# Two more 8 KB load tiles in a hybrid layer kernel, room taken from GpSimd's descriptor ring and from small tiles

## The chip, the cores and the metric

The kernel runs on one core of one Trainium2 chip. The metric is device time in microseconds (us) of one launch. Engines are called by the profile's names: PE (TensorE, with PEld for its weight loads), DVE (VectorE), ACT (ScalarE), POOL (GpSimd) and SP (SyncE, which here only issues DMAs). All weights lie in device memory as float32 and are read once.

## The reference

One layer of a diffusion backbone over 512 latent tokens and 256 context tokens of width 1024. Cut to what matters:

```
m  = silu(c) @ w_mod + b_mod                       # 6 vectors: shift, scale, gate, twice
h  = rmsnorm(x, g1) * (1 + scale1) + shift1        # the same for ctx
u  = h @ w_in                                      # q, k, v (512 each) | hyena (768) | conformer (512)
na = neighbourhood_attention(q, k, v, k_ctx, v_ctx, rpb)   # 8 heads, 8x16 window + 256 context keys
hy = hyena_mixer(u_hy)                             # short conv, two long convs by FFT, gates
cf = conformer_conv(u_cf)                          # GLU, 31-tap conv, layer norm, silu
x  = x + gate1 * (concat(na, hy, cf) @ w_out)
h  = rmsnorm(x, g2) * (1 + scale2) + shift2
# 16 experts, each takes its top 64 tokens by softmax affinity
aff = softmax(h @ w_router);  gate, idx = top_k(aff.T, 64)
y_e = (silu(h[idx] @ w1[e]) * (h[idx] @ w3[e])) @ w2[e]    # 1024 -> 2048 -> 1024
x  = x + gate2 * scatter_add(gate * y_e, idx)
out = rmsnorm(x, final_norm_g)
```

## The kernel before

**Load tiles.** A pool `big` holds `NU` = 22 tiles of 128 partitions x 2048 float32 (8 KB a partition, 1 MB in all). Every weight piece is loaded into such a tile, and many intermediate results (rows of x, the halves of split weights, mixer outputs `mixh`, `mixl`, the bias table `tm`) take one too. `U()` (L65) hands a tile out; a counter `used` may not go over `NU`. The loads stand in one list, `loads`, in a fixed order: adaLN and input-projection pieces by a string of letters (L227), the two halves of the k projection, then `w_out` and the rows of x (L252), adaLN group 3 (L259), and from L261 on for each expert eight pairs `w1`, `w3` and eight `w2`. `pump` (L72) issues from the head of that list while fewer than `NU` tiles are in use (less a reserve, `keep`); it is called where the code gives tiles back (`free`). All of these loads go out from SP's one queue in this order (`load`, L162). Since the pool goes round, a load waits on the chip for the last readers of the tile that it gets.

**Stages.** (1) to about 96 us: adaLN groups and the transposed, normalised x. (2) 96 to 262 us: the input projections. For exactness, weights and activations are split into a high and a low float32r part (`split`: ACT L515 makes `wh`; POOL or DVE, L516, makes `wl`), and three products are summed on PE (`mm3`, L548 to L550). Between them lie the hyena mixer (PE L698 in the DFT's space, DVE L685 to L707, POOL L685) and the conformer branch (DVE L583 GLU, L590 the 31-tap conv in 60 instructions, then the layer norm whose first matmuls are PE `pL` L598, and DVE `mixl` L562 at its end). (3) Attention: scores (PE `pS` L932, DVE L940, ACT L943), transposes (L952), values (L963), with the output projection's matmuls (`pX`) and routing laid between by a written order of PE's instructions. The keys `KK` are copied out of PSUM by L105 (DVE) and L103 (ACT). The upper half of `w_out` is multiplied by the gate vector `g1bc` on DVE (L867, four instructions a tile) as it comes in. The bias table is made by POOL (L849) from pieces that POOL itself loads (`fetch_bias`, L841). (4) The experts: PE L1305 and L1306 (`pa`, w1 and w3), L1333 transposes, L1346 (`py`, w2); gather and scatter are matmuls too (L1182, L1202). (5) The end: last scatter, final norm, output by 4 DMAs and one indirect DMA of POOL for the rows of the last expert (L1373).

In stages 1 and 2 a scheduler sets the order of instructions on each engine; its order depends on when it thinks a load arrives. From the start of attention on, PE's order is written out by hand.

Of the kernel before, what the change touches and what calls it, by code (L numbers as in the profile page):

```python
# [9 lines left out]
FT = mybir.dt.float32  # L10
FR = mybir.dt.float32r
I32 = mybir.dt.int32
U32 = mybir.dt.uint32
# [9 lines left out]
CAP = 64  # L23
FF = 2048
EPS = 1e-6
NU = 22
RPBW = 63


# [21 lines left out]
def hybrid_kernel(ctx: ExitStack, tc: tile.TileContext, a, out: bass.AP):  # L51
    nc = tc.nc
# [59 lines left out]
    ident = c1[:, C1["id"]]  # L112
    bmod = early.tile([32, 512], FT, name="bmod")
    nc.scalar.dma_start(bmod, a["bmod"])
    eps = small.tile([128, 1], FT, name="eps")
    nc.vector.memset(eps, EPS)
    one256 = small.tile([128, 1], FT, name="one256")
    nc.vector.memset(one256, 1.0 / 256.0)
    ones = one256.to_broadcast([128, 128])
    g1bc = small.tile([128, D], FT, name="g1bc")  # L120
# [12 lines left out]
    pair = small.tile([128, 64], FT, name="pair")  # L133
    nc.vector.tensor_add(pair, ident[:, 0:64], ident[:, 64:128])

    def small_t(name, n, dt=FT, bufs=4):
        return work.tile([128, n], dt, name=name, tag=name, bufs=bufs)

    def rsqrt_mean(dst, ss, n, scale=1.0 / D):
# [127 lines left out]
            load(("w2", e, j), a["w2"][e, j * 256:(j + 1) * 256].rearrange("(p k) n -> p (k n)", k=2))  # L267


    def norm_rows(rows, junk, n, ss, name):  # L270

        for i in range(n):
            nc.scalar.activation(junk[i], rows[i], AF.Square, accum_out=ss[:, i:i + 1])
        rs = small.tile([128, n], FT, name=name)
        rsqrt_mean(rs, ss[:, :n], n)
        for i in range(n):
            nc.vector.tensor_scalar(rows[i], rows[i], rs[:, i:i + 1], None, op0=OP.mult)
# [50 lines left out]
    nc.vector.tensor_sub(h2s[64:128], h2f[64:128], h2s[64:128].bitcast(FT))  # L328
    free_only(1)
    xn = [take(("x", 0)), take(("x", 1))]  # L330
    ss = small.tile([128, 4], FT, name="ssx")
    hr = [U("hr0"), U("hr1")]
    pump(6)
    half = lambda t, i: t[:, i * D:(i + 1) * D]
    norm_rows([half(xn[b // 2], b % 2) for b in range(4)], [half(hr[b // 2], b % 2) for b in range(4)], 4, ss, "rsx")

    def transpose_rows(src, n, dst):

# [437 lines left out]
    def ctx_prep():  # L776
        cx = take("ctx")
        rows = [half(cx, i) for i in range(2)]
        ssc = small.tile([128, 2], FT, name="ssc")
        hcr = U("hcr")  # L780
        norm_rows(rows, [half(hcr, i) for i in range(2)], 2, ssc, "rsc")
        yield
        v256 = hcr.rearrange("p (k n) -> p k n", n=256)
        for _ in transpose_rows(rows, 2, lambda k4, i: v256[:, 4 * k4:4 * k4 + 4, 128 * i:128 * i + 128]):
            pass
        free_only(1)
        yield
        cmod = modulate_split(lambda k: v256[:, k], 256, 1, "hc")
        kv["hc"] = next(cmod)
        finish(cmod)  # L790
        free_only(1)
        yield
# [123 lines left out]
    xblk = lambda b: xr[b // 2][:, (b % 2) * D:(b % 2 + 1) * D]  # L916

    tok = c1[:, C1["tok"]]
    ssq = small.tile([128, 4, 2], FT, name="ssq")

    affT = g1bc[0:16, 0:512].rearrange("e (i n) -> e i n", i=2)
    idxf = p1[0:16, 0:128].rearrange("e (i n) -> e i n", i=2)
    rsT = small.tile([128, 4], FT, name="rsT")

    def scores(hp, b):

        k0 = 8 * KB[b]
        o = 768 * (hp % 2) + k0
        kk = KK[hp // 2][:, o:o + 2 * (512 - k0)].rearrange("p (a n) -> p a n", a=2)[:, :, 0:256]
        pss = [psA("pS") for _ in range(2)]  # L930
        for s in range(2):
            mm(pss[s].rearrange("p (a n) -> p a n", a=2), Q[0][HALF[s], hp, 128 * b:128 * b + 128], kk[HALF[s]],  # L932
               start=True, stop=True)
        out = []
        for s, ps in enumerate(pss):
            p = W("P")
            i = 2 * TYPE[b] + s
            m2 = small_t("m2", 4, bufs=6)

            nc.vector.tensor_tensor_reduce(out=p.rearrange("p (a n) -> p a n", a=2), in0=ps.rearrange("p (a n) -> p a n", a=2),  # L940
                                           in1=TM[hp][:, i:7:6 - i], scale=1.0, scalar=3e38,
                                           op0=OP.add, op1=OP.min, accum_out=m2[:, 0:1])
            nc.scalar.activation(p, p, AF.Exp, scale=-1.0, bias=m2[:, 0:1], accum_out=m2[:, 1:2])  # L943
            nc.vector.reciprocal(m2[:, 2:3], m2[:, 1:2])
            nc.vector.tensor_scalar(p, p, m2[:, 2:3], None, op0=OP.mult)
            out.append(p)
        return out
# [68 lines left out]
    def route(b):  # L1016
        eng = nc.vector if b in () else nc.gpsimd
        s1 = small_t("s1", 1)
        eng.tensor_add(s1, ssq[:, b, 0:1], ssq[:, b, 1:2])
        rs = rsT[:, b:b + 1]  # L1020
        v, t, y = small_t("rv", 1), small_t("rt", 1), small_t("ry", 1, I32)
        yf = y.bitcast(FT)
        eng.tensor_scalar(v, s1, 1.0 / D, EPS, op0=OP.mult, op1=OP.add)
        eng.tensor_scalar(y, v.bitcast(I32), -0.5, 1597463007.0, op0=OP.mult, op1=OP.add)
        eng.tensor_scalar(v, v, -0.5, None, op0=OP.mult)
        for i in range(3):
            eng.tensor_scalar(t, yf, yf, v, op0=OP.mult, op1=OP.mult)
            eng.tensor_scalar(rs if i == 2 else yf, t, 1.5, yf, op0=OP.add, op1=OP.mult)
        x_rows(b, 1)
        yield  # L1030
        pl = psY("pR")
        for k4 in range(2):
            for k in range(4):
                mm(pl[32 * k:32 * k + 32, 0:128], rwA[:, 4 * k4 + k], xTr[b, k4][:, k * 128:(k + 1) * 128],
                   start=(k4 == 0), stop=(k4 == 1))
        lt = W("lt")[:, 0:128]
        nc.scalar.activation(lt, pl[:, 0:128], AF.Copy)
        yield
        p2 = psY("pR")
        mm(p2[:, 0:16], lt, rsum, start=True, stop=True)  # L1040
        lg = small_t("lg", 16, bufs=2)
        nc.vector.scalar_tensor_tensor(lg, p2[:, 0:16], rs, rwB, op0=OP.mult, op1=OP.add)

        mx = small_t("mx", 1)
        nc.vector.tensor_reduce(out=mx, in_=lg, axis=AX.X, op=OP.min)
        ex = small_t("ex", 16, bufs=2)
        sm_ = small_t("sme", 2)
        nc.scalar.activation(ex, lg, AF.Exp, scale=-1.0, bias=mx, accum_out=sm_[:, 0:1])
        nc.vector.reciprocal(sm_[:, 1:2], sm_[:, 0:1])
        nc.vector.tensor_scalar(ex, ex, sm_[:, 1:2], None, op0=OP.mult)  # L1050
        yield
        p3 = psY("pR")
        nc.tensor.transpose(p3[0:16, 0:128], ex, ident)
        c = slice(16 * (b % 2), 16 * (b % 2) + 16)
        nc.vector.tensor_copy(affT[:, b // 2].rearrange("e (r c) -> e c r", c=32)[:, c], cr(p3[0:16, 0:128]))
# [169 lines left out]
    pi = psY("pI")  # L1225
    nc.tensor.transpose(pi[:, 0:16], idxf.rearrange("e a b -> e (a b)"), ident[0:16, 0:16])
    nc.tensor.transpose(pi[:, 16:32], vals.rearrange("e a b -> e (a b)"), ident[0:16, 0:16])
    fng = rwA.rearrange("p k e -> p (k e)")[0:8, 0:128]
    ig = small.tile([128, 32], FT, name="ig")
    nc.vector.tensor_copy(ig, pi[:, 0:32])  # L1230
    nc.gpsimd.dma_start(fng, a["fng"].rearrange("(r p) -> r p", p=128))
    prev = None
# [2 lines left out]

    def final_rows():

        s2 = small.tile([128, 4, 2], FT, name="s2")
        s1 = small.tile([128, 4], FT, name="s1f")
        rs = small.tile([128, 4], FT, name="rsf")  # L1240
        e = E - 1
        pb = psY("pB")
        mm(pb[:, 0:64], ident[0:16, e:e + 1].to_broadcast([16, 128]), idxf[:, 0], start=True, stop=True)
# [12 lines left out]
        for h in range(2):  # L1256
            p = psT("pB")
# [9 lines left out]
        for h in range(2):  # L1267
            nc.vector.tensor_add(pairs[:, 64 * h:64 * h + 64], ident[:, 0:64], ident[:, 64:128])

        where = small.tile([128, 4], U32, name="where")  # L1270
        nc.vector.tensor_copy(where[:, 0:1], ig[:, e:e + 1])
        for i, (bits, shift) in enumerate(((31, 1), (224, 2))):
            nc.vector.tensor_scalar(where[:, i + 1:i + 2], where[:, 0:1], bits, shift,
# [195 lines left out]
```

## Time and profile before

| what | value |
|---|---|
| time, median of 3 runs | 1343.46 us (1341.08 to 1345.36) |
| profiled execution: its own time | 1341.92 us |
| profiled execution: span of the trace | 1340.1 us |
| mean granted TensorE clock | 0.985 |
| PE busy | 1255.4 us (94%) |
| DVE, ACT, POOL busy | 505.7, 223.9, 156.5 us |
| DMA traffic | 457.99 MB, mean 342 GB/s |

The span is what the trace covers; 1.8 us lie around it. A busy share is an average over the whole span: PE's 94% says only that few stages leave it idle, not that PE sets the end of each. In the strip of 40 slices below, one slice is 33.5 us long.

### The profile page before, as it was taken

What the parts mean: (1) busy time and instruction counts of PE and PEld (TensorE: products, weight loads), DVE (VectorE), ACT (ScalarE), POOL (GpSimd) and SP (SyncE); (2) the same over time, 40 slices, a digit from 0 to 9 for tenths busy, and PEclk for the clock granted to TensorE, in tenths of its full rate; (3) what the DMA queues carried; (4) which work ended last, traced back from release to release, by engine and by line L of the source; (5) the groups of instructions that cost most, each with busy time, mean ns of one, the idle gap of its engine ahead of it and who ended that gap; (6) DMA issues with size and microseconds to landing.
All of it is one profiled execution on the core that took longest, in us unless ns stands there. A gap on an engine that the chain in (4) does not pass through costs nothing.

```text
span 1340.1 us, 14779 instructions
## 1 busy us (share of the span) xinstructions
PE 1255.4 (94%) x5916; PEld 578.9 (43%) x5916; DVE 505.7 (38%) x1034; ACT 223.9 (17%) x480; POOL 156.5 (12%) x166
## 2 busy tenths in 40 slices
PE   6898988989979999999999999999999999999997
PEld 2576567856644333333333334343333334343332
DVE  6877998478571131221312122121211212121224
ACT  3532232335520110101101011010101001010103
POOL 2333444546110000000000000000000000000000
PEclk9998999989989999999999999999999999999999
DMA  9934214534367999999999999999999999999996
GB/s 344 375 138 162 77 63 118 190 127 185 139 270 276 421 422 421 422 421 421 421 420 420 422 421 421 421 421 421 421 421 421 422 421 421 421 421 422 421 420 256
DMA packets 72979, 457.99 MB, mean 342 GB/s; under 512 B 7364, under 2 KB 9228, under 8 KB 21710
## 3 DMA queue, kind: packets, MB, share of 16 engines
q1 hardware_dynamic: 71662, 453.64, 83.4%
q0 software_dynamic: 912, 3.06, 0.9%
q8 instruction: 46, 0.75, 0.2%
q10 hardware_dynamic: 336, 0.35, 0.1%
q14 instruction: 23, 0.19, 0.0%
HBM read 453.87 MB, written 2.36 MB: 340 GB/s over the span
## 4 chain that ended last, share of the span: by engine, by line
PE 49%; DMA 35%; DVE 13%; issue 2%; ACT 1%; POOLq 0%; SPq 0%; DVEq 0%; ACTq 0%
DMA ld<-in_w_dram 33%; PE pa L1305 18%; PE py L1346 7%; DVE glu L590 4%; PE pZ L1202 3%; PE pG L1182 2%; PE pP L550 1%; PE pP L548 1%; PE pP L549 1%; PE pS L932 1%; PE pO L963 1%; PE pM L431 1%; PE pX L548 1%; PE pX L549 1%; PE pX L550 1%
## 5 line engine op out<-in xcount | busy, mean ns | idle before, releaser
L1306 PE MATMUL pa<-ld,xh 128*64 128x512 f32 x1024 | 463.8, 597 | 14.7 <-DMA ld<-in_w_dram 14.7
L1305 PE MATMUL pa<-ld,xh 128*64 128x512 f32 x1024 | 466.4, 597 | 0.3 <-DVE xh L1062 0.3
L1346 PE MATMUL py<-ld,xh 128*64 128x512 f32 x1024 | 223.3, 594 | 0.0
L1305 PEld LDWEIGHTS pa<-ld,xh 128*64 128x64 f32 x1024 | 131.6, 136 | 199.1 <-issue 191.2
L1205 DVE TENSOR_TENSOR acc<-acc,pZ 128x512 f32<-128x512 f32 x112 | 73.2, 685 | 288.7 <-PE pZ L1202 288.2
L1306 PEld LDWEIGHTS pa<-ld,xh 128*64 128x64 f32 x1024 | 132.2, 137 | 102.5 <-issue 65.1
L1346 PEld LDWEIGHTS py<-ld,xh 128*64 128x64 f32 x1024 | 72.1, 137 | 139.3 <-issue 136.9
L1373 POOL DMA_INDIRECT out_dram<-yg,where x1 | 1.1, 1097 | 932.0 <-DVE yg L1372 932.0
L1060 ACT ACTIVATE xh<-pT,B,A 128x64 f32<-128x64 f32 (+1 forms) x60 | 24.4, 406 | 443.1 <-PE pT L1190 334.3
L1350 DVE SCALAR_TENSOR_TENSOR yg<-py,ig,g1bc 128x512 f32<-128x512 f32 x16 | 12.0, 752 | 205.0 <-PE py L1346 205.0
L1202 PE MATMUL pZ<-yg,oh 64*128 64x512 f32 x240 | 84.4, 640 | 4.8 <-DVE acc L1205 3.9
L516 POOL TENSOR_TENSOR wl<-ld,wh 128x512 fp32r<-128x512 f32 x44 | 64.5, 1493 | 81.7 <-ACT wh L515 42.0
L548 PE MATMUL pP<-hh,wh 128*128 128x512 f32 x144 | 59.0, 411 | 1.2 <-ACT hh L505 1.2
L550 PE MATMUL pP<-hh,wl 128*128 128x512 f32 x144 | 57.2, 405 | 2.7 <-DVE wl L516 2.7
L549 PE MATMUL pP<-hl,wh 128*128 128x512 f32 x144 | 57.0, 397 | 1.5 <-DVE hl L507 1.5
L590 DVE SCALAR_TENSOR_TENSOR glu<-glu,p 128x512 f32<-128x512 f32 x60 | 56.9, 949 | 1.1
L1333 PE MATMUL pT<-c,au 128*128 128x128 f32 x256 | 47.4, 312 | 6.2 <-DVE xh L1336 2.2
L1182 PE MATMUL pG<-ld,ohg 128*64 128x512 f32 x224 | 52.8, 592 | 0.0
L1202 PEld LDWEIGHTS pZ<-yg,oh 64*128 64x128 f32 x240 | 22.7, 184 | 65.6 <-issue 35.7
L103 ACT ACTIVATE xg<-pG 128x512 f32<-128x512 f32 x7 | 4.2, 597 | 279.3 <-PE pG L1182 279.3
L1062 DVE TENSOR_SCALAR xh<-pT,A,B 128x64 f32<-128x64 f32 (+1 forms) x60 | 20.7, 344 | 73.5 <-ACT xh L1060 28.5
L1333 PEld LDWEIGHTS pT<-c,au 128*128 128x128 f32 x256 | 35.7, 208 | 26.9 <-DVE acc L1205 12.5
(345 smaller groups left out, 1353.7 us busy)
## 6 DMA issues: line engine op xcount, KB each, us to landing
ld<-in_w_dram SPq DMA_DIRECT2D x384, 1024.0 KB, 19.8
ld<-in_w_mod_dram SPq DMA_DIRECT2D x24, 1024.0 KB, 14.2
ld<-in_w_in_dram SPq DMA_DIRECT2D x11, 1024.0 KB, 5.5
ld<-in_w_out_dram SPq DMA_DIRECT2D x4, 1024.0 KB, 5.1
ld<-in_x_dram SPq DMA_DIRECT2D x2, 1024.0 KB, 12.4
ld<-in_x_dram SPq DMA_DIRECT2D x4, 512.0 KB, 6.7
out_dram<-acc SPq DMA_DIRECT2D x4, 512.0 KB, 9.3
g<-in_rpb_dram POOLq DMA_DIRECT2D x8, 244.5 KB, 6.1
```

Of the source, the lines that this page charges most:

```text
L516: (nc.vector if i in dve else nc.gpsimd).tensor_sub(lo[:, s], raw[:, s], hi[:, s].bitcast(FT))
L548: mm(ps, l[0], r[0], start=start, stop=False)
L549: mm(ps, l[0], r[1], start=False, stop=False)
L550: return mm(ps, l[1], r[0], start=False, stop=stop)
L590: nc.vector.scalar_tensor_tensor(yc[i], glt[i][:, j:j + 512], cw[:, i, j:j + 1], yc[i], op0=OP.mult, op1=OP.add)
L1182: mm(pg[64 * h:64 * h + 64], g[:, 64 * b:64 * b + 64], xblk(b)[:, 512 * h:512 * h + 512], start=(b == 0), stop=(b == 3))
L1202: mm(ps[h], oh[pr, 128 * c:128 * c + 128], yg[pr], start=True, stop=True)
L1205: nc.vector.tensor_add(ablk(c)[:, s], (ablk if e else xblk)(c)[:, s], ps[h])
L1305: mm(pa[f][0:64], xT[:, k, cs], w1[:, s], start=(k == 0), stop=(k == 7))
L1306: mm(pa[f][64:128], xT[:, k, cs], w3[:, s], start=(k == 0), stop=(k == 7))
L1333: nc.tensor.transpose(p[:, i * 128:(i + 1) * 128], au[f][:, c:c + 255:2], ident)
L1346: mm(py[64 * h:64 * h + 64], hT[:, f], w2[:, i * 1024 + 512 * h:i * 1024 + 512 * h + 512], start=(f == 0), stop=(f == 15))
```

## The change

The pool gets 24 tiles instead of 22. Room for the 16 KB comes from four places: the ring in which GpSimd writes the descriptors of its own DMAs is set to 1 KB a partition; single-column statistics go into one array `stat` (128x32) or into unused columns of `rwA`, where each had a tile of its own; small scalar tiles have 2 buffers instead of 4 (`m2` 5 instead of 6); and the router's exponentials are written over the logits.

```diff
-NU = 22
+NU = 24
...
-    eps = small.tile([128, 1], FT, name="eps")
+    stat = small.tile([128, 32], FT, name="stat")
+    eps, one256 = stat[:, 0:1], stat[:, 1:2]
...
-    def small_t(name, n, dt=FT, bufs=4):
+    def small_t(name, n, dt=FT, bufs=2):
...
-    ss = small.tile([128, 4], FT, name="ssx")
+    ss = stat[:, 4:8]
...
-    ssq = small.tile([128, 4, 2], FT, name="ssq")
+    ssq = stat[:, 16:24].rearrange("p (b n) -> p b n", n=2)
...
-            m2 = small_t("m2", 4, bufs=6)
+            m2 = small_t("m2", 4, bufs=5)
...
-        ex = small_t("ex", 16, bufs=2)
+        ex = lg
...
-    fng = rwA.rearrange("p k e -> p (k e)")[0:8, 0:128]
-    ig = small.tile([128, 32], FT, name="ig")
+    rwf = rwA.rearrange("p k e -> p (k e)")
+    fng, ig = rwf[0:8, 0:128], rwf[:, 128:160]
...
-        s2 = small.tile([128, 4, 2], FT, name="s2")
-        s1 = small.tile([128, 4], FT, name="s1f")
-        rs = small.tile([128, 4], FT, name="rsf")
+        s2 = rwf[:, 160:168].rearrange("p (c h) -> p c h", h=2)
+        s1, rs = rwf[:, 168:172], rwf[:, 172:176]
...
-    nc = _bacc.Bacc("TRN2", target_bir_lowering=False, num_devices=1)
+    nc = _bacc.Bacc("TRN2", target_bir_lowering=False, num_devices=1, dynamic_dma_scratch_size=1024)
```

Each engine has the same instructions as before, in the same number. The order differs in stage 2 and at its border with attention. Lines of the changed kernel are one lower there (L866 is L867 of before).

At the start of attention, DVE before; `ld` is a `w_out` tile, `pC` and `pP` hold the keys of the context and of the latent tokens:

```order
L618 TENSOR_TENSOR glu<-glu,pL 128x512 x2
L105 COPY KK<-pC 128x256
L562 TENSOR_TENSOR mixl_1175<-glu,mixh_1174 128x512 x2
L105 COPY KK<-pC 128x256
L105 COPY KK<-pP 128x512
L867 TENSOR_TENSOR ld<-ld,g1bc 128x512 x8
L105 COPY KK<-pP 128x512
```

DVE at the same place in the changed kernel:

```order
L617 TENSOR_TENSOR glu<-glu,pL 128x512 x2
L866 TENSOR_TENSOR ld<-ld,g1bc 128x512 x4
L561 TENSOR_TENSOR mixl_1172<-glu,mixh_1171 128x512
L105 COPY KK<-pC 128x256
L561 TENSOR_TENSOR mixl_1172<-glu,mixh_1171 128x512
L105 COPY KK<-pC 128x256
L866 TENSOR_TENSOR ld<-ld,g1bc 128x512 x4
L105 COPY KK<-pP 128x512 x2
```

The first tile's four gate products now stand ahead of `mixl`, the second tile's four after it; both copies of the latent keys still end the group.

SP's queue at the `w_out` loads, before; in brackets stand the semaphores waited for (DMAHW ones are SP's own lanes, the others name the engine that read the tile last):

```order
L162 DMA ld<-in_w_out_dram 128x4x512 [waits DVE_49]
L162 DMA ld<-in_w_out_dram 128x4x512 [waits DMAHW3_49,PE_49,Pool_49]
L162 DMA ld<-in_w_out_dram 128x4x512 [waits DMAHW4_49,PE_49]
L162 DMA ld<-in_w_mod_dram 128x2x1024 [waits DMAHW5_49,PE_49]
L162 DMA ld<-in_w_mod_dram 128x2x1024 [waits DMAHW6_49,PE_49]
```

The same five loads in the changed kernel:

```order
L162 DMA ld<-in_w_out_dram 128x4x512 [waits DMAHW2_49,PE_49]
L162 DMA ld<-in_w_out_dram 128x4x512 [waits DMAHW3_49,PE_49]
L162 DMA ld<-in_w_out_dram 128x4x512 [waits DVE_49,DMAHW4_49,PE_49,Pool_49]
L162 DMA ld<-in_w_mod_dram 128x2x1024 [waits DMAHW5_49,PE_49]
L162 DMA ld<-in_w_mod_dram 128x2x1024 [waits DMAHW6_49,DVE_49]
```

The wait for DVE that stood ahead of the first of three `w_out` loads now stands ahead of the third.

In stage 2, DVE before, around the first long conv of the hyena branch (L687 to L689 finish the spectrum `Y`, L516 makes a low half of a weight):

```order
L685 TENSOR_TENSOR t<-pH,KM 128x512 x2
L516 TENSOR_TENSOR wl<-ld,wh 128x512 x2
L687 TENSOR_TENSOR t<-t 128x512 x2
L640 SCALAR_TENSOR_TENSOR hx<-u,p_70,hx 128x511
L687 TENSOR_TENSOR t<-t 128x512
L688 TENSOR_TENSOR Y<-t 128x256
L689 TENSOR_TENSOR Y<-t 128x256
```

The changed kernel there:

```order
L515 TENSOR_TENSOR wl<-ld,wh 128x512 x2
L684 TENSOR_TENSOR t<-pH,KM 128x512 x2
L639 SCALAR_TENSOR_TENSOR hx<-u,p_70,hx 128x511
...
L640 SCALAR_TENSOR_TENSOR hx<-u,p_70,hx 128x511
L686 TENSOR_TENSOR t<-t 128x512 x2
L687 TENSOR_TENSOR Y<-t 128x256
```

The two `wl` stand ahead of the products with `KM` now, and the first `Y` follows its two L686 directly. PE's order in stage 2 moved with it: four more projection matmuls stand ahead of the L698 group that needs this `Y`, and the second `pL` (L598) stands 13 matmuls earlier among the projections.

## Rows read from the trace of the kernel before

**Rows 1.** The page: GB/s in 40 equal slices of the span.

```profile
GB/s 344 375 138 162 77 63 118 190 127 185 139 270 276 421 422 421 422 421 421 421 420 420 422 421 421 421 421 421 421 421 421 422 421 421 421 421 422 421 420 256
```

**Rows 2.** The page: the chain that ended last, by engine.

```profile
PE 49%; DMA 35%; DVE 13%; issue 2%; ACT 1%; POOLq 0%; SPq 0%; DVEq 0%; ACTq 0%
```

**Rows 3.** Windows: PE, PEld, DVE, ACT, POOL busy, granted clock, DMA share, GB/s.

```profile
400.00:442.00 42.00, 40.32 (x204) 18.13 (x204) 7.92 (x32) 2.43 (x5) 1.05 (x1) 1.00 0.72 285
...
835.00:1276.00 441.00, 423.90 (x1810) 162.18 (x1810) 85.47 (x174) 31.81 (x76) 0.00 (x0) 1.00 1.01 421
```

**Rows 4.** Issues of SP's queue from 395 us on, and median issue to landing.

```profile
411.00 56.72 SPq L162 DMA_DIRECT2D ld<-in_w_dram  x27
...
ld<-in_w_dram SPq DMA_DIRECT2D x384, 1024.0 KB, 19.8
```

**Rows 5.** PE's timeline at its last wait for a weight of the experts.

```profile
1275.97 0.64 PE L1306 MATMUL pa<-ld,xh 128*64 128x512 f32 x1 [1.32 <-DMA ld<-in_w_dram]
```

**Rows 6.** The chain from 215 to 300 us, into attention: start, us, what.

```profile
225.99 0.68 DVE vc L105
226.67 0.60 DVE wl L516
...
233.23 0.23 PE pP L550
...
252.52 12.21 DMA ld<-in_w_out_dram
```

**Rows 7.** DVE's timeline from 248 to 271 us.

```profile
248.87 2.59 DVE L562 TENSOR_TENSOR mixl<-glu,mixh 128x512 fp32r<-128x512 f32 x2
...
260.75 2.50 DVE L867 TENSOR_TENSOR ld<-ld,g1bc 128x512 f32<-128x512 f32 x4 [2.78 <-DMA ld<-in_w_out_dram]
264.75 5.38 DVE L867 TENSOR_TENSOR ld<-ld,g1bc 128x512 f32<-128x512 f32 x4 [1.49 <-DMA ld<-in_w_out_dram]
270.06 0.68 DVE L105 COPY KK<-pP 128x512 f32<-128x512 f32 x1
```

**Rows 8.** SP: issue of the last `w_out` loads, their wait, their median to landing.

```profile
251.49 1.47 SPq L162 DMA_DIRECT2D ld<-in_w_out_dram  x3
...
SPq L162 <- DVE mixl L562: 30.9, 1, 30.9
...
ld<-in_w_out_dram SPq DMA_DIRECT2D x4, 1024.0 KB, 5.1
```

**Rows 9.** PE's timeline at the start of attention.

```profile
262.61 1.13 PE L932 MATMUL pS<-KK,Q 64*128 64x512 f32 x4
...
266.31 0.39 PE L550 MATMUL pX<-wh,mixl 128*128 128x512 f32 x1
270.79 2.68 PE L932 MATMUL pS<-KK,Q 64*128 64x512 f32 x4 [4.09 <-DVE KK L105]
```

**Rows 10.** The window behind that wait, columns as in rows 3.

```profile
270.80:277.50 6.70, 6.70 (x19) 4.61 (x20) 5.90 (x18) 3.52 (x9) 0.33 (x1) 0.53 0.28 75
```

**Rows 11.** PE's waits from 96 to 265 us: sum, times, longest.

```profile
PE pH L698 <- DVE Y L688: 4.3, 2, 3.9
PE pL L598 <- DVE glu L590: 3.4, 1, 3.4
```

**Rows 12.** Windows behind those two waits, columns as in rows 3.

```profile
109.80:116.60 6.80, 5.85 (x19) 3.29 (x20) 3.34 (x11) 0.00 (x0) 0.01 (x1) 0.50 0.51 168
229.20:232.70 3.50, 3.50 (x18) 3.40 (x17) 2.31 (x4) 1.26 (x2) 0.00 (x0) 0.51 0.00 0
```

**Rows 13.** DVE's timeline from 126 to 135 us, in the conformer branch.

```profile
126.69 1.07 DVE L583 TENSOR_TENSOR glu<-pP,sig 128x512 f32<-128x512 f32 x1 [3.14 <-PE pP L550]
...
132.52 1.77 DVE L516 TENSOR_TENSOR wl<-ld,wh 128x512 fp32r<-128x512 f32 x1
```

**Rows 14.** GpSimd's own DMAs: the page's queue row, and POOL's timeline behind two loads.

```profile
q0 software_dynamic: 912, 3.06, 0.9%
...
249.41 3.38 POOL L849 TENSOR_TENSOR tm<-c,g 128x256 f32<-128x256 f32 x3 [2.53 <-DMA g<-in_rpb_dram]
```

More of the change, by code (lines that the diff above doesn't have):

```diff
@@ L114, in hybrid_kernel @@
     nc.scalar.dma_start(bmod, a["bmod"])
-    eps = small.tile([128, 1], FT, name="eps")
+    stat = small.tile([128, 32], FT, name="stat")
+    eps, one256 = stat[:, 0:1], stat[:, 1:2]
     nc.vector.memset(eps, EPS)
-    one256 = small.tile([128, 1], FT, name="one256")
     nc.vector.memset(one256, 1.0 / 256.0)
@@ L267, in hybrid_kernel, with norm_rows @@
             load(("w2", e, j), a["w2"][e, j * 256:(j + 1) * 256].rearrange("(p k) n -> p (k n)", k=2))
-    def norm_rows(rows, junk, n, ss, name):
+    def norm_rows(rows, junk, n, ss, rs):
         for i in range(n):
             nc.scalar.activation(junk[i], rows[i], AF.Square, accum_out=ss[:, i:i + 1])
-        rs = small.tile([128, n], FT, name=name)
         rsqrt_mean(rs, ss[:, :n], n)
@@ L334, in hybrid_kernel @@
     half = lambda t, i: t[:, i * D:(i + 1) * D]
-    norm_rows([half(xn[b // 2], b % 2) for b in range(4)], [half(hr[b // 2], b % 2) for b in range(4)], 4, ss, "rsx")
+    norm_rows([half(xn[b // 2], b % 2) for b in range(4)], [half(hr[b // 2], b % 2) for b in range(4)], 4, ss, stat[:, 8:12])
     def transpose_rows(src, n, dst):
@@ L778, in ctx_prep @@
         rows = [half(cx, i) for i in range(2)]
-        ssc = small.tile([128, 2], FT, name="ssc")
+        ssc = stat[:, 12:14]
         hcr = U("hcr")
-        norm_rows(rows, [half(hcr, i) for i in range(2)], 2, ssc, "rsc")
+        norm_rows(rows, [half(hcr, i) for i in range(2)], 2, ssc, stat[:, 14:16])
         yield
@@ L918, in hybrid_kernel @@
     tok = c1[:, C1["tok"]]
-    ssq = small.tile([128, 4, 2], FT, name="ssq")
+    ssq = stat[:, 16:24].rearrange("p (b n) -> p b n", n=2)
     affT = g1bc[0:16, 0:512].rearrange("e (i n) -> e i n", i=2)
     idxf = p1[0:16, 0:128].rearrange("e (i n) -> e i n", i=2)
-    rsT = small.tile([128, 4], FT, name="rsT")
+    rsT = stat[:, 24:28]
     def scores(hp, b):
@@ L1268, in final_rows @@
             nc.vector.tensor_add(pairs[:, 64 * h:64 * h + 64], ident[:, 0:64], ident[:, 64:128])
-        where = small.tile([128, 4], U32, name="where")
+        where = rwf[:, 176:180].bitcast(U32)
         nc.vector.tensor_copy(where[:, 0:1], ig[:, e:e + 1])
```

## The prediction

> **What bounds the kernel now.** I read the page first: the strip of GB/s holds 420 to 422 from about 440 us to the end [rows 1], and the chain that ended last is PE's for 49% and DMA's for 35% [rows 2]. So there are two regimes, and a busy share of 94% for PE does not tell them apart; windows do. From about 440 us on the DMA engines are full (share 1.01 at 421 GB/s in the long window), between 400 and 442 us they are at 0.72 [rows 3]. The reader is to see where that loss lies: SP's queue starts its next stretch of issues at 411.0 us [rows 4], when the experts' first matmuls give the first tiles back; all tiles were full until then. One load of 1024 KB at 421 GB/s takes 1,048,576 / 421,000 = 2.49 us, and a load lands 19.8 us after its issue [rows 4], which is eight of these: SP has eight under way at all times. In the last such stretch, 835 to 1276 us, PE is busy 423.90 of 441 us while DMA is full [rows 3]: 17.1 us are lost to weights that come late. The last wait of that kind ends at 1275.97 us [rows 5]; after it PE's own work, some 64 us of last expert and final norm, sets the end. So the end hangs on: start of the experts + (loads not yet made then) x 2.49 us.
>
> Ahead of the experts the chain runs through PE, DVE and a few loads, and there I looked for waits that hang on a tile. The chain from 215 to 300 us shows one: 12.21 us of a `w_out` load, with DVE's products of that tile behind it [rows 6]. SP had waited 30.9 us for DVE's `mixl` (L562) before it could issue that load, at 251.49 us, with two more right behind [rows 8]. DVE waits for the tiles 2.78 and 1.49 us, multiplies them in 2.50 and 5.38 us, and only then copies the last keys, at 270.06 us [rows 7]. PE, whose score matmul stood ready at 262.61 us and whose fill-in work ended with the `pX` matmul of 266.31 us, stands 4.09 us for that copy [rows 9], and the next 6.70 us run at a granted clock of 0.53 [rows 10].
>
> **The change, part by part.** *Two tiles at the start of the experts.* With 24 tiles each load waits for the readers that, before, the load two places ahead of it waited for. Before the experts all tiles are full in both kernels, so two more of the 384 expert loads are in when DMA becomes the bound: 2 x 2.49 = 4.98 us fewer. The gain passes on as long as PE loses at least that much to late weights: it loses 17.1 us in the one window, so it does, whole. Bounds: 4.98 above; nothing below, if DMA had another limit in 411 to 442 us. I take 4.98.
>
> *The stall at the start of attention.* In the changed kernel the first two of the three `w_out` loads no longer wait for `mixl`; the third does. That third one, issued when `mixl` is done, is the only thing still late, so I follow it. DVE's group is now four L867, `mixl`, a key copy, four L867, two key copies. If the first four run as the first group did (2.50 us) and begin where `mixl` did at 248.87 us, `mixl` ends at 248.87 + 2.50 + 2.59 = 254.0; with the slower row (5.38) at 256.8. The load lands 5.1 us behind [rows 8]: 259.1 or 261.9. Four L867 more, quick or slow, 261.6 or 267.3, and two copies of 0.68 us: 262.9 or 268.7. PE has `pX` work until about 266.7. So of the 4.09 us between none and 2.0 stay. With no gap, or a short one, I expect no half clock behind it: that window cost 6.70 x (1 - 0.53) = 3.15 us. The whole is 4.09 + 3.15 = 7.24 us; the bounds are 7.24 and, if 2.0 us of gap and the low clock stay, 2.1. I take 7.24, since what is slow needs POOL's table work to fall on both groups, and only one of two did before.
>
> *Stage 2.* Here the order on PE, DVE and POOL moved, for the scheduler expects other loads. Two waits of PE matter: 3.9 us for `Y` of the hyena branch, 3.4 for the end of the 31-tap conv [rows 11]. Behind each the clock is about half: 5.85 us busy at 0.50, 3.50 us at 0.51 [rows 12]. What leads to the second wait is DVE's conv, which runs without idle from the GLU at 126.69 us on, with a `wl` of 1.77 us between its taps [rows 13]. Two such `wl` now stand ahead of the GLU, in 3.14 us of idle [rows 13], and a key copy with a short `wl` moved behind the conv (0.68 + 0.60 in the chain [rows 6]): the conv ends up to 2 x 1.77 + 1.28 = 4.8 us earlier. Against it, the second `pL` now stands 13 projection matmuls (0.23 us each [rows 6], 3.0 us) further up, so that work comes behind the wait. If both hold: 4.8 - 3.0 = 1.8 us gained. Best end: the conv's 4.8 and half of the 3.50 us at low clock, 6.6 us. Worst end: the conv is no earlier, the 3.0 us come on top. The first wait, for `Y`, is filled by four matmuls more (0.9 us); since the conv stands on DVE behind its own chain, I give it nothing beyond that range. I take 1.8.
>
> *The smaller scalars.* Statistics in one array, two buffers instead of four, exponentials in place: every reader and writer of these stands on the same instruction and waits for the same one as before, so I price it at nothing. The cover is that the columns are apart; if `stat` made its readers wait for one another, three of them in line would cost, at the 0.68 us of a far larger copy [rows 7], 2.0 us at most.
>
> *The ring.* GpSimd makes the descriptors for 16 DMAs, 912 packets or 57 to each of the 16 DMA engines over the whole run [rows 14]; at most two of its loads are under way at once. No row shows GpSimd waiting for room. Nearest row: a wait of 2.53 us for such a load to land [rows 14]; if one DMA had to wait for the one ahead, this is its price. Taken: nothing. The Trainium skill ("Perfetto Trace Analysis", section "DMA Instruction — SWDGE (GPSIMD)") speaks against the change here: DMA engines may begin before all descriptors are written above all when more are generated than the buffer holds, so that generation then goes at the pace at which the engines drain it. By that rule, the price would stand on GpSimd's issue instructions; no run here shows a buffer that is full.
>
> **The sum**, against the profiled run: 1341.92 - 4.98 - 7.24 - 1.8 = 1327.9 us. The median of the runs lies 1.54 us over the profiled one; from there it is 1329.4. I say 1329.
>
> **The rivals.** (1) *Stage 2 gives its best end as well*, or loses its half clock at both places: 1341.92 - 4.98 - 7.24 - 6.6 = 1323.1. For it: four matmuls into the gap for `Y`, `wl` out of the taps. Against: the earlier `pL`. (2) *Only the tiles pay.* The stall goes but PE stands elsewhere for the same, for instance for POOL's table or the earlier `pL`: 1341.92 - 4.98 = 1336.9, by the median 1338.5. For it: DVE and POOL hold each other up (2.50 against 5.38 us for the same four), and both groups are still there. (3) *The change does not do what it says*: what is loaded earlier was hidden anyway, or stage 2 loses its 3.0 and the low clock stays; with 2.1 from the stall and nothing from the tiles 1341.92 - 2.1 + 3.0 = 1342.8, no change. Against: 17.1 us of late weights. (4) *Slower: the ring.* 14 of GpSimd's DMAs stand ahead of or in attention. If each waits 2.53 us for room, POOL comes 14 x 2.53 = 35.4 us later to its `wl` and its table, for which PE waits in turn. Slower begins where more than 14.0 + 4.0 = 18 of these 35.4 us reach PE; with all of it 1327.9 + 35.4 = 1363.3, with two thirds 1351.5. For it: PE reads POOL's `wl` and, through DVE, its table. Against: 57 packets an engine in 250 us.
>
> **Chances.** My forecast (from 1326 to 1333) 0.54; rival 1 0.13; rival 2 0.15; rival 3 0.10; rival 4 0.08. A measurement of this kernel tells about 0.3%, 4.0 us, from no change. Faster: 0.54 + 0.13 and 0.14 of rival 2, whose 1336.9 to 1338.5 lies 5 us below the median: 0.81. Same: 0.11. Slower: 0.08. The range takes in rivals 1 and 2 and leaves out 3 and 4: 1322 to 1339.
>
> **What would show it.** Right: SP's next stretch of issues begins with the experts, with two more of the expert loads issued before it; the last wait of L1306 for a weight comes about 14 us earlier; no wait of the score matmul for `KK` above 2 us and a granted clock near 1 in the 7 us behind it; two of the three `w_out` loads issued before 230 us. Wrong: a wait of PE for `pL` longer than 4.6 us with a long half clock; POOL's issue instructions of 3 us instead of 0.5; a DMA share under 1 after the first expert; or the low clock of 0.5 at a new place, since each such stretch costs 1.7 to 3.2 us.

## The result, and the profile after

The changed kernel takes 1328.57 us (median of 4 runs, 1326.90 to 1329.64) against 1343.95 us (1341.08 to 1345.36): ratio 0.9887, 95% interval 0.9871 to 0.9902. That is 15.4 us, or 1.1%. The profiled execution took 1326.90 us with a span of 1325.1 us, 15.0 us less than the span of before.

The page of the changed kernel, its strip of GB/s and the chain by engine, to be set beside [rows 1, 2]:

```profile
GB/s 347 393 177 185 5 69 179 225 154 159 141 241 380 419 418 419 420 420 419 419 420 419 420 420 420 419 419 420 419 420 419 420 419 419 420 420 420 418 420 263
...
PE 56%; DMA 27%; DVE 14%; issue 2%; ACT 1%; POOLq 0%; SPq 0%; DVEq 0%; ACTq 0%
```

The thirteenth slice already holds 380 GB/s where it held 276. The chain's share of DMA tells little: it is 27% here and 35% before, but 50% in e1 below, which takes the time of before. Windows of the changed kernel (columns as in rows 3):

```profile
400.00:442.00 42.00, 40.22 (x200) 17.71 (x200) 4.21 (x9) 5.28 (x10) 0.00 (x0) 0.96 1.00 412
442.00:500.00 58.00, 56.94 (x258) 19.45 (x256) 12.33 (x25) 4.14 (x10) 0.00 (x0) 1.00 1.01 418
...
835.00:1261.00 426.00, 413.17 (x1764) 154.83 (x1762) 84.32 (x172) 31.35 (x74) 0.00 (x0) 0.99 1.01 420
```

In 400 to 442 us the DMA share is 1.00 where it was 0.72 [rows 3]: the experts began at 393.61 us instead of 406.09. Of the 426 us before the last late weight PE loses 12.8, where it lost 17.1 of 441. That last late weight, in PE's timeline (start, us, what, idle before):

```profile
1260.81 0.64 PE L1304 MATMUL pa<-ld,xh 128*64 128x512 f32 x1 [1.33 <-DMA ld<-in_w_dram]
```

It comes 15.2 us earlier than in [rows 5].

At the start of attention, PE's and DVE's timelines of the changed kernel, to be set beside [rows 9] and [rows 7]:

```profile
257.39 1.13 PE L931 MATMUL pS<-KK,Q 64*128 64x512 f32 x4
...
261.41 1.13 PE L931 MATMUL pS<-KK,Q 64*128 64x512 f32 x4
```

```profile
239.65 5.38 DVE L866 TENSOR_TENSOR ld<-ld,g1bc 128x512 f32<-128x512 f32 x4
244.95 1.61 DVE L561 TENSOR_TENSOR mixl<-glu,mixh 128x512 fp32r<-128x512 f32 x1
...
252.85 2.48 DVE L866 TENSOR_TENSOR ld<-ld,g1bc 128x512 f32<-128x512 f32 x4
...
257.50 0.69 DVE L105 COPY KK<-pP 128x512 f32<-128x512 f32 x1 [1.57 <-PE pP L549]
```

```profile
257.00:262.00 5.00, 5.00 (x23) 2.81 (x21) 3.69 (x9) 1.52 (x4) 4.70 (x7) 1.00 1.01 407
```

The second row of score matmuls follows its fill-in work with no idle time, the granted clock is 1.00, and now DVE waits for PE (1.57 us) instead of PE for DVE. SP's queue: the last three `w_out` loads leave at 211.26, 212.25 and 243.63 us, where the first of them had left at 251.49 [rows 8]; the row gives them together:

```profile
211.26 32.73 SPq L162 DMA_DIRECT2D ld<-in_w_out_dram  x3
```

PE's waits of the changed kernel ahead of attention (sum, times, longest), and windows behind the one for `Y` (the same stretch as in rows 12) and around the one for the 31-tap conv, to be set beside [rows 11, 12]:

```profile
PE pL L597 <- DVE glu L589: 3.9, 1, 3.9
PE pH L697 <- DVE Y L687: 2.1, 2, 1.5
```

```profile
109.80:116.60 6.80, 6.80 (x46) 5.33 (x45) 4.67 (x11) 1.32 (x3) 0.00 (x0) 1.00 0.65 247
219.00:223.00 4.00, 3.59 (x8) 2.37 (x9) 3.96 (x11) 0.05 (x1) 0.00 (x0) 0.50 1.03 328
```

The wait for `Y` fell from 3.9 to 1.5 us and no low clock stands behind it any more. The wait for the conv did not shorten (3.9 us against 3.4), and its low clock of 0.50 stayed.

To compare executions, I cut each into five stretches at the first `pK` matmul (about 29 us in), the first `pS`, the first and the last `pO`, the first `pa`, and the end; each number is the difference of two starts in PE's timeline. "Issued" counts the expert loads that SP had issued at the first `pa`.

| kernel | issued | pK to pS | pS to pO | pO to pO | pO to pa | pa to end |
|---|---|---|---|---|---|---|
| before | 20 | 233.54 | 16.28 | 95.54 | 31.65 | 934.05 |
| after | 22 | 228.54 | 8.85 | 95.55 | 31.82 | 931.51 |
| e1: 22 tiles | 20 | 232.46 | 15.60 | 95.62 | 31.66 | 937.29 |
| e2: tiles for experts | 22 | 234.90 | 15.42 | 95.53 | 31.66 | 933.10 |
| e3: keys first | 20 | 232.35 | 9.83 | 113.72 | 31.69 | 937.33 |
| e4: held 1 us | 22 | 228.47 | 8.85 | 95.52 | 31.82 | 931.89 |
| e6: held 10 us | 22 | 227.66 | 10.97 | 95.42 | 31.70 | 933.21 |
| e7: 23 tiles | 21 | 227.34 | 10.02 | 95.57 | 31.69 | 934.42 |
| e8: v low on DVE | 22 | 224.03 | 14.65 | 95.53 | 31.70 | 931.93 |
| e9: held from w_out | 20 | 227.83 | 9.44 | 95.61 | 31.89 | 937.15 |
| e10: held from attention | 20 | 228.46 | 8.86 | 97.72 | 34.12 | 939.71 |
| e11: e8, keys on ACT | 22 | 222.70 | 12.93 | 95.55 | 31.89 | 932.07 |
| e12: 22 tiles, keys on ACT | 20 | 235.18 | 15.00 | 95.58 | 31.66 | 937.05 |

The fifth kernel has no line: its profiled execution was disturbed, so its times alone are used. From before to after the columns give -5.00, -7.43, +0.01, +0.17 and -2.54 us; with a first `pK` 0.22 us earlier that is the 15.0.

### The profile page after: what moved, and what is told of

The parts are those of the page before. It is cut to its first block, busy times and chain, and to the rows that moved or that the text cites. A ratio compares the mean times of both kernels' runs of the same rounds, so it can differ in the third digit from the quotient of the medians.

```text
span 1325.1 us, 14788 instructions
## 1 busy us (share of the span) xinstructions
PE 1251.3 (94%) x5916; PEld 569.6 (43%) x5916; DVE 509.0 (38%) x1034; ACT 224.1 (17%) x480; POOL 157.5 (12%) x166
## 3 DMA queue, kind: packets, MB, share of 16 engines
q0 software_dynamic: 912, 3.06, 0.8%
## 4 chain that ended last, share of the span: by engine, by line
PE 56%; DMA 27%; DVE 14%; issue 2%; ACT 1%; POOLq 0%; SPq 0%; DVEq 0%; ACTq 0%
DMA ld<-in_w_dram 26%; PE pa L1303 20%; PE py L1344 8%; DVE glu L589 4%; PE pZ L1201 4%; PE pa L1304 3%; PE pG L1181 2%; PE pT L1331 1%; PE pP L549 1%; PE pP L548 1%; PE pP L547 1%; PE pS L931 1%; PE pO L962 1%; PE pX L547 1%; PE pX L549 1%
## 5 line engine op out<-in xcount | busy, mean ns | idle before, releaser
L1344 PE MATMUL py<-ld,xh 128*64 128x512 f32 x1024 | 224.2, 596 | 0.0
L1348 DVE SCALAR_TENSOR_TENSOR yg<-py,rwA,g1bc 128x512 f32<-128x512 f32 x16 | 12.0, 750 | 206.0 <-PE py L1344 206.0
L1331 PE MATMUL pT<-c,au 128*128 128x128 f32 x256 | 51.3, 336 | 5.5 <-DVE xh L1334 2.2
## 6 DMA issues: line engine op xcount, KB each, us to landing
ld<-in_x_dram SPq DMA_DIRECT2D x2, 1024.0 KB, 12.8
```

The lines of the kernel that those rows point to most:

```text
L1331: nc.tensor.transpose(p[:, i * 128:(i + 1) * 128], au[f][:, c:c + 255:2], ident)
L1344: mm(py[64 * h:64 * h + 64], hT[:, f], w2[:, i * 1024 + 512 * h:i * 1024 + 512 * h + 512], start=(f == 0), stop=(f == 15))
```

## The experiments

The theory was that three parts add up: two loads of head start for the experts (4.98 us), the stall at the start of attention (7.24) and the order of stage 2; ring and scalars nothing. Before was timed again beside each group of experiments, with medians of 1344.01 (e1 to e4), 1342.51 (e5 to e8) and 1343.62 us (e9 to e12).

**e1: everything but the tiles.**

```diff
-NU = 24
+NU = 22
```

> The changed kernel with 22 tiles again: ring of 1 KB, statistics in one array, fewer scalar buffers, exponentials in place, but no more room for loads. Its PE, POOL and SP orders are those of the kernel before. Theory (these edits cost nothing, all of the gain is the tiles): the kernel before within 0.2%, GpSimd's DMA issues at 0.5 us as before. Rival (the small ring or shared scalars cost time that the two tiles hide): slower than before by 2.5 us or more, with longer issues on POOL or new DVE waits. Second rival (the edits themselves are part of the gain): faster by 3 us or more.

1343.92 us against 1344.01, ratio 1.0005 (0.9996 to 1.0015): no difference to 0.15%. GpSimd's loads go out as before, POOL's timeline:

```profile
244.26 1.03 POOL L840 DMA_DIRECT2D g<-in_rpb_dram  x2 [0.92 <-PE pL L615]
248.07 3.13 POOL L848 TENSOR_TENSOR tm<-c,g 128x256 f32<-128x256 f32 x3 [2.77 <-DMA g<-in_rpb_dram]
```

Two issues in 1.03 us, and 2.77 us of wait for the load as in [rows 14] (2.53). A ring of 1 KB, shared statistics and fewer buffers together cost nothing that the time shows: by the interval between 0.5 us less and 2.0 us more. Rival 4 of the prediction falls with it.

**e2: two tiles for the expert loads alone.** Every twelfth expert load goes to a second pool of two tiles; the first use of each waits for the last key copy.

```diff
+            if count[0] % 12 == 4:
+                t = big2.tile([128, 2048], FT, name="ld", tag="V")
+                if count[0] < 24:
+                    nc.gpsimd.tensor_copy(t[:, 0:1], KK[1][:, 0:1])
```

> 22 tiles as in the first kernel, and two more from a pool of their own that serve the expert loads alone, from the start of attention on (each waits first for the last key copy). PE's order is that of the kernel before throughout. Theory (two loads fewer left when the experts start, 2.49 us each): 5.0 us faster than before. Rival by the profile of the changed kernel, in which the time from the first expert matmul to the end shrank by 2.5 us and the loads came 2.472 us apart where they came 2.465 us before: a gain of 2.5 us, again with the slower spacing. Neither changes the 4.09 us wait of the score matmul.

1341.66 us, ratio 0.9978 (0.9969 to 0.9987): 2.3 us by the median, as the rival said. The table says more: from the first expert matmul on, it is 4.2 us shorter than e1 (933.10 against 937.29). In this pair of executions that was hidden: the experts of e2 began 4.4 us later (408.31 against 403.91), half of it because its first `pK` came at 30.80 us and not at 28.57, the rest in stage 2 (234.90 against 232.46), where e12, with the same order, took 235.18. The profiled execution of e2 (1343.19 us) also lies 1.5 us over its median. So the median and the trace don't agree on the size.

**e3: the key copies ahead of the gate products, with 22 tiles.** Ahead of each tile's products, one small DVE instruction reads the last key copy and writes the first column of the gate values back unchanged, so that the products come behind the copies.

```diff
+            gt = g1bc[:, n * 512:n * 512 + 1]
+            nc.vector.scalar_tensor_tensor(gt, KK[1][:, 768:769], 0.0, gt, op0=OP.mult, op1=OP.add)
```

> 22 tiles as in the first kernel; the products of w_out with the gate vector are made to wait for the last key copy (one small DVE instruction between that writes back what it read of the gate vector), so that DVE copies the keys first. PE's order is that of the kernel before. Theory (the stall at the start of attention came from what stood ahead of the key copy on DVE, not from the tiles as such): 7.2 us faster than before, no wait of the score matmul above 1 us, clock near 1 behind it, while the w_out loads are as late as before. Rival (DVE's wait only moves: the products now hold up the first row minima of the scores): 0 to 2 us faster.

1361.47 us, ratio 1.0118 (1.0100 to 1.0136): 16 us slower by the ratio, 17.5 by the medians. The stall itself went as the theory had it, 9.83 us from `pS` to `pO` where e1 has 15.60. But the stretch behind it, 95.5 us in every other kernel but e10, took 113.7. DVE's timeline of e3 shows where the products went:

```profile
284.92 6.23 DVE L868 TENSOR_TENSOR ld<-ld,g1bc 128x512 f32<-128x512 f32 x4
...
302.29 0.69 DVE L941 CUSTOM_DVE_ANT_1 P<-pS,tm 128x512 f32<-128x512 f32 x1 [6.46 <-PE pS L933]
```

and its PE waits from 255 to 420 us, and a window behind them:

```profile
PE pO L964 <- DVE PT L105: 8.2, 2, 6.4
PE pO L964 <- ACT PT L103: 4.9, 2, 4.6
```

```profile
295.00:305.00 10.00, 10.00 (x46) 3.70 (x46) 2.24 (x8) 1.43 (x4) 0.82 (x2) 0.67 0.67 217
```

The first four stand in the middle of attention, where PE waits for DVE's results, and take 6.23 us while POOL is busy; PE waits 6.4 us for one copy behind them, and runs at a clock of 0.67 after it. Neither theory nor rival had the place to which the scheduler would move them.

**e4 and e5: two tiles taken away late.** Both are the changed kernel with two `pad` tiles, taken after attention (e4) and in its middle (e5), and read once at the end of the program.

```diff
+                pads = [U("pad0"), U("pad1")]
+                for p_ in pads:
+                    nc.gpsimd.memset(p_[:, 0:1], 0.0)
...
+    nc.vector.tensor_copy(pads[0][:, 0:1], pads[1][:, 0:1])
```

> The changed kernel, with two tiles taken out of the pool at the end of attention and kept to the end, so that the experts load into 22. PE's order is that of the changed kernel. Theory: the experts' share is 5.0 us, so slower than the changed kernel by 5.0 us, 10 us faster than before, with the experts starting when they do in the changed kernel. Rival: the experts' share is 2.5 us, 12.5 us faster than before.

> The changed kernel, with two tiles taken out of the pool in the middle of attention (where the second part of the output projection gives back its four) and kept to the end. The fourth kernel took them too late: 22 expert loads had been issued when the experts started, as in the changed kernel. Here it should be 20, as before. PE's order is that of the changed kernel. Theory (the two loads ahead at the experts' start are the gain there, 2.49 us each): 5.0 us slower than the changed kernel, about 1333.5. Rival (worth what the second kernel gained over the first, 2.3): about 1331. Rival (worth nothing, as the fourth kernel seems to say): about 1328.6.

1328.83 us (ratio 0.9889, 0.9874 to 0.9905) and 1328.40 us (0.9894, 0.9877 to 0.9912): as the changed kernel. That looked like the end of the head start, but the experiments did not do what they were for. The trace of e4, asked for the pads:

```profile
L1130 POOL MEMSET pad<- x2: 99/99/99, 365.0 to 365.2; 128x1 f32 x2
L1362 DVE COPY pad<-pad x1: 160/160/160, 366.0 to 366.0; 128x1 f32<-128x1 f32 x1
```

The read that should have kept the tiles needed nothing but the two memsets, so the scheduler ran it 1 us after them, and the tiles went back. In e4 22 loads were out when the experts began, as in the changed kernel. The pads of e5 went the same way (memsets up to 314.2 us, the read at 316.1). The two count as repeats of the changed kernel, within 0.3 us of its median.

**e6: the same slip with tiles taken ahead of the `w_out` loads.** The pads stand ahead of `pump(3)`; they were held from 214.4 to 224.2 us.

> The changed kernel, with the two tiles taken out of the pool just ahead of the w_out loads and kept to the end: stage 2 runs in the changed kernel's order (6 matmuls of PE moved by one place), but DVE has its eight gate products again between the last two key copies, and the experts load into 22. Theory (the order in stage 2 gives 5.2 us by itself, the end of the key projection being that much earlier in the changed kernel's trace; the stall and the head start are lost): 1343.9 - 5.2 = 1338.7. Rival (stage 2 gives nothing by itself, its 5.2 us is how executions differ): 1343.9. Rival (stall goes without the tiles, since two of the three w_out loads still wait for PE alone): 1338.7 - 7 = 1331.5.

1330.24 us, ratio 0.9904 (0.9888 to 0.9919). It tells one thing. DVE has all eight products between the last two key copies, as before:

```profile
252.04 8.81 DVE L869 TENSOR_TENSOR ld<-ld,g1bc 128x512 f32<-128x512 f32 x8
260.79 0.68 DVE L105 COPY KK<-pP 128x512 f32<-128x512 f32 x1
```

but its `w_out` loads are issued from 236.26 us on, so DVE starts them at 252.04 without a wait, and PE waits 0.7 us for the copy instead of 4.09: this order on DVE does not make the stall by itself.

**e7: 23 tiles.**

```diff
-NU = 24
+NU = 23
```

> The changed kernel with 23 tiles. One load of head start (2.5 us), a stage 2 with before's place of the second pL and another order around it, four gate products instead of eight ahead of the last key copy. Theory (three separate gains, of which this has half of the first, little of stage 2 and part of the stall's 7.2): 1334 to 1340. Rival (the gain is the number of tiles, in proportion): 1336.2, with the stage-2 order of no account.

1332.63 us, ratio 0.9919 (0.9902 to 0.9936). One tile gives about two thirds of the gain: all of stage 2 (227.34), most of the stall (10.02), and one load of head start (934.42 lies between 937 and 932). So stage 2's gain is a matter of the order that comes out, not of a count; the theory's steps hold, its guess "little of stage 2" does not.

**e9: tiles really held, from the `w_out` loads to the end.** The read now depends on the last result.

```diff
+    for p_ in pads:
+        nc.vector.tensor_copy(p_[:, 0:1], yg[:, 0:1])
```

> The changed kernel, with two tiles taken out of the pool just ahead of the w_out loads and now really kept to the end (in the fourth to sixth kernel the read that was to keep them could run at once, so they were held for 1 to 10 us and those kernels are the changed one again, the sixth with later w_out loads). PE's order is that of the changed kernel, the first w_out load waits for DVE's mixl again, the experts load into 22. Theory (three parts; only stage 2's order, 4 to 5 us, is left): about 1339. Rival (stage 2 gives nothing): 1343.9. Rival (w_out and head start matter little, as the sixth and e2 seem to say): 1331 to 1333.

1336.64 us, ratio 0.9956 (0.9944 to 0.9968): 7.0 us gained by the medians, 5.9 by the ratio. 20 loads are issued at the experts' start, and from there the end is 937.15 us away, as in e1, e3 and e12 (937.05 to 937.33). Stage 2 takes 227.83. The surprise is 9.44 us from `pS` to `pO`: the stall did not come back although the first of the three `w_out` loads waits for `mixl` and leaves at 245.38 us. DVE has its eight products between the last two key copies, as before:

```profile
252.93 0.69 DVE L105 COPY KK<-pP 128x512 f32<-128x512 f32 x1 [4.97 <-PE pP L549]
253.89 2.50 DVE L869 TENSOR_TENSOR ld<-ld,g1bc 128x512 f32<-128x512 f32 x4 [0.27 <-DMA ld<-in_w_out_dram]
257.21 3.06 DVE L869 TENSOR_TENSOR ld<-ld,g1bc 128x512 f32<-128x512 f32 x4 [0.82 <-DMA ld<-in_w_out_dram]
260.20 0.68 DVE L105 COPY KK<-pP 128x512 f32<-128x512 f32 x1
```

The loads leave 12.9 us ahead of the first `pS` (258.26) where they left 11.1 ahead before, and the second group takes 3.06 us and not 5.38. The last copy comes 1.9 us behind `pS`, inside PE's 4 us of fill-in work; before it was 7.5 us behind. With the stage-2 order of the changed kernel, then, the stall mostly goes even with late loads and with DVE's order of before; the early loads add at most 0.6 us to that (8.85 against 9.44).

**e10: tiles held from the middle of attention to the end.** As e5, with e9's read.

> The changed kernel with two tiles taken out in the middle of attention and really kept to the end. PE's order is that of the changed kernel, the w_out loads are early, 20 expert loads are issued when the experts start instead of 22. Theory (head start, 2 x 2.49 us): 5.0 us slower than the changed kernel, about 1333.5; with the tail's PE as the bound for a part of it, as in the second kernel, 2.3 to 4.2 us slower, 1331 to 1333. Rival (nothing): 1328.6. The step from the kernel with tiles held from w_out on to this one is the stall: theory 7 us.

1338.94 us, ratio 0.9950 (0.9931 to 0.9968), 10 us slower than the changed kernel and not 5, and 2.3 us slower than e9, where theory had it 7 us faster. The seven runs do not agree: 1332.59 and 1334.76 us, then 1337.85 to 1339.86; the profiled one is the longest. Its window ahead of the experts:

```profile
385.00:405.00 20.00, 16.93 (x57) 8.24 (x58) 10.19 (x46) 0.46 (x1) 1.05 (x1) 0.74 0.01 5
```

The clock is 0.74, where the changed kernel has 0.95 in 380 to 400 us and 1.00 from 385 on. The table has 2.2 us more than the changed kernel from the first to the last `pO`, 2.3 more from `pO` to `pa`, and, from `pa` to the end, 2.5 more than the other kernels with 20 loads; the first expert load after `pa` leaves 6.9 us behind it and not 4.9. Together 7.0 us: with the 4.9 of the head start, 11.9 of the 12.3 us by which this execution is longer than that of the changed kernel. What brings the clock down there, and whether the other long runs lose the same, is not shown.

**e8, e11 and e12: trying for more, and where the wait sits.** e8 has half of the low parts of the `v` weights on DVE; e11 has also all copies of the latent keys on ACT; e12 has the key copies on ACT with 22 tiles.

```diff
-    DVE_LO = {('q', 0): (0, 2), ...
+    DVE_LO = {('v', 0): (0, 2), ('v', 1): (1, 3), ('q', 0): (0, 2), ...
...
-                    copy(kat(m)[:, 0:512], pss[m])
+                    nc.scalar.activation(kat(m)[:, 0:512], pss[m], AF.Copy)
```

> The changed kernel with half of the low parts of the v weights made by DVE instead of POOL. PE then has the second pL 30 matmuls later among its projections (6.9 us of work at 0.23 us) and POOL runs beside fewer taps of the conv. Theory (PE's 3.9 us wait for the conv and the low clock behind it are what stage 2 still loses): 3 to 6 us faster than the changed kernel, about 1324. Rival (the conv's chain on DVE is the bound and gets seven low parts more of 0.7 to 1.8 us each): no faster, up to 5 us slower.

> The eighth kernel (half of v's low parts on DVE, 24 tiles) with all four copies of the latent keys on ACT. In the eighth PE reached attention 4.6 us earlier than in the changed kernel and lost it to a 2.3 us wait for the last key copy, behind four gate products on DVE, and a half clock behind that. Theory (the copy was what PE waited for): 4 to 5 us faster than the changed kernel, about 1324. Rival (DVE's row minima stand behind the same gate products, so PE waits for them instead): 1328 to 1329.

> The first kernel (22 tiles, order of before) with all four copies of the latent keys on ACT: the w_out loads are late as before, DVE waits for them as before, but PE need not wait for DVE's copy. Theory (the stall is DVE's, blocked by a late load: row minima and with them the exponentials and transposes come after the gate products all the same): 0 to 3 us faster than before. Rival (the key copy alone made the stall): 7.2 us faster, about 1336.7, which would make 24 tiles unneeded for that part.

e8: 1328.78 us, ratio 0.9893 (0.9874 to 0.9911), as the changed kernel. Stage 2 is 4.5 us shorter (224.03), and all of it is lost again behind `pS` (14.65 against 8.85): the wait for the key copy is back at 2.3 us, since the third `w_out` load is as late as ever (243.48 us against 243.63). e11: 1327.12 us, ratio 0.9874 (0.9854 to 0.9895), against 0.9887 for the changed kernel; the intervals overlap, so it is not shown to be faster. From `pS` to `pO` it still takes 12.93 us, with a wait of 0.6 us for the row minima, which is nearer to the rival than to the theory. e12: 1343.63 us, ratio 0.9998 (0.9985 to 1.0011): nothing gained with 22 tiles. PE's waits of e12 from 262 to 285 us, and a window:

```profile
PE pS L931 <- DVE m L939: 1.8, 1, 1.8
```

```profile
272.00:280.00 8.00, 8.00 (x36) 5.74 (x36) 5.98 (x14) 2.68 (x7) 1.38 (x2) 0.62 0.29 75
```

PE waits for the row minima instead of the copy, 1.8 us, and the low clock follows all the same. So the copy was only the first thing that stood behind DVE's late products.

## Why the prediction was right, point by point

**The sum.** 1329 was forecast, 1328.57 measured. One term was too small: in stage 2 the first rival came nearer than the forecast, though not in the time; the others did not come true.

**Ring and scalars, nothing:** right within e1's interval. The Trainium skill ("Perfetto Trace Analysis", section "DMA Instruction — SWDGE (GPSIMD)") says that DMA engines may begin before the last descriptor is written, particularly when more are generated than the descriptor buffer holds. That generation then goes at their pace and shows in POOL's issues is the prediction's own inference; each of the 16 issues in e1 took the time that it took before, to 0.01 us, so no run here shows that case. That at most two of GpSimd's loads are under way at once holds for the bias table alone: of the copies `vodd`, four are issued within 1.6 us in e1 and land 2.7 us after their issue, by the median.

**The head start, 4.98 us:** right by the traces of the experiments, though the two profiled executions of before and after alone show 2.54. Four executions with 20 loads issued (e1, e3, e9, e12; e10 with its 939.71 is left out) lie at 937.05 to 937.33 us from the first expert matmul to the end, six with 22 (after, e2, e4, e6, e8, e11) at 931.51 to 933.21: means 937.2 and 932.3, a difference of 4.9, with e7's 21 loads between. The profiled execution of before is the odd one out with 934.05. Its loads came faster: from 500 to 1250 us its packets make 421.1 GB/s, and those of the twelve other executions in the table 419.4 to 419.6; over 900 us such a difference is 3.4 us, enough for the 3.1 us by which it falls short of the other four. Whether that belongs to this one execution or to the kernel before is not shown, for it was traced once, and it is the only kernel here with the large ring; e1 bounds only what ring and scalars cost together. By medians e2 shows 2.3 of the 4.9; the rest of that one is open, so the size is shown by this stretch of the traces and not by times.

**The stall, 7.24 us:** the size was right (7.43 between the two profiles; 16.28, 15.60, 15.42 and 15.00 with it, 8.85 or 8.86 without it in the changed kernel, e4 and e10). The reason was half right. The prediction has the third `w_out` load issued when `mixl` is done; in the changed kernel its wait for DVE was over at 221.3 us, it then stood 22.3 us for a context-key matmul of PE (`pC`), and left at 243.63, ahead of `mixl` (244.95). It had landed when DVE came to it at 252.85, so the late tile that the prediction followed was not late there. It is not the copy's place on DVE (e12) and the products cannot simply be moved (e3); it is that DVE's products come too late for PE's cover. The prediction put their coming in time down to the early loads; with stage 2's new order the late loads just suffice too (e9), and no kernel here has early loads with the order of before. So what early loads do by themselves is not shown; with the new order, all but 0.6 us of this term is there without them.

**Stage 2, 1.8 us:** too small; it is 5.0 between the two profiles, and the kernels stand apart by more than their spread: 232.35 to 235.18 us with the order of before (before, e1, e2, e3, e12), 227.66 to 228.54 with the new one (after, e4, e6, e9, e10). The step that failed is "since the conv stands on DVE behind its own chain, I give it nothing" for the wait for `Y`. Three pieces show it, from the first `pK` to the GLU ahead of the conv, from there to the second `pL`, and on to the first `pS`. Before:

```profile
29.07 1.96 PE L392 MATMUL pK<-sm,ld 128*128 128x512 f32 x4 [0.42 <-PE pM L431]
...
227.99 1.12 PE L598 MATMUL pL<-glu,one 128*128 128x512 f32 x2 [3.42 <-DVE glu L590]
```

The changed kernel:

```profile
28.85 1.96 PE L391 MATMUL pK<-sm,ld 128*128 128x512 f32 x4 [0.42 <-PE pM L430]
...
122.27 1.09 DVE L582 TENSOR_TENSOR glu<-pP,sig 128x512 f32<-128x512 f32 x1
...
219.41 2.08 PE L597 MATMUL pL<-glu,stat 128*128 128x512 f32 x2 [3.92 <-DVE glu L589]
```

The GLU of before began at 126.69 us and had waited 3.14 us for PE [rows 13], so it moves with PE: it came 4.2 us earlier (122.27 - 28.85 against 126.69 - 29.07), 1.2 of it ahead of PE's group that had waited for `Y`, and 3.0 between this group and the GLU, where the half clock had stood. The conv to `pL` took 97.14 us instead of 101.30, 4.2 us less, where the prediction had priced 4.8; from `pL` to `pS` it took 3.4 us more (37.98 against 34.62), where it had priced 3.0. So the two priced pieces gave 0.8 us, and the piece that was put at nothing gave 4.2. e7 shows it by itself: there the conv to `pL` takes 101.43 us, as before, and the GLU begins 92.78 us behind `pK` instead of 97.62, behind a wait for `Y` of 1.5 us. The worst end, +3.0, had the sign wrong; the best end, -6.6, would have been the better guess.

**Where the two errors met.** Between the two profiles stage 2 gave 3.2 us more than forecast, and the experts 2.4 us less, since those of before ran faster than in any other kernel with 20 loads. The close hit on the time owes something to that. With the head start of the experiments the three parts make 5.0 + 7.4 + 4.9 = 17.3 us, 1.9 more than the medians show; where that goes is open.

## What to carry to other kernels

Two more buffers in a loading pool were worth here, in a DMA-bound stretch behind one in which the DMA engines were not full, about two transfers: 4.9 us from the start of that stretch, against 2 x 2.49. In a kernel whose order is made by a scheduler the larger effect was the new order: read the places where one engine waits for another, and ask of each wait whether its engine moves when the one ahead does. A delay put on one engine to free another must be followed to the place where it lands, as e3 shows; and an experiment that holds a resource must be seen to hold it in the trace.

## What the runs showed of the hardware

In one execution of the changed kernel, the same four gate products on DVE took 2.48 us with POOL idle (at 252.85 us) and 5.38 us with POOL's table work beside them for 4.91 us (at 239.65); in e3 they took 6.23 us with POOL busy throughout. All kernels here have the same 58 matmul instructions ahead of the first `pK`, and yet it came at 28.57 us in one execution and at 30.80 in another; and one execution of thirteen moved its loads at 421.1 GB/s where the others had 419.4 to 419.6, 3 us in 900. Both are as large as single terms of this sum, so a pair of profiles does not settle a term below 3 us.
